# Softmax bias, scale and running minimum in one VectorE instruction per head, statistics of the last block one step later, last squares summed by TensorE

## The chip, the cores and the metric

The kernel runs on one core of a Trainium2 chip. The metric is the device time of one execution in microseconds (us). The engines are TensorE (PE in the profile, with PEld for its weight loads), VectorE (DVE), ScalarE (ACT), GpSimd (POOL) and SyncE (SP), which issues most of the transfers.

## The reference

One decoder layer on x of 2048 tokens by 1024 features, with three parallel mixers and a squared-ReLU MLP:

```python
proj = rmsnorm(x, norm1) @ w_in          # q|k|v|B|C|hc|p, 1792 columns
# attention, 8 heads of 64, 2 key heads, window 128, queries in blocks of 128
scores = einsum('bnqhgd,bnkhd->bnhgqk', qb, k_band) * scale        # 256 keys a block
scores = where(valid, scores + bias, NEG)
m = maximum(max(scores, axis=-1), sink)
p = exp(scores - m)
probs = p / (sum(p, axis=-1) + exp(sink - m))
attn = einsum('bnhgqk,bnkhd->bnqhgd', probs, v_band)
x = x + concat(attn, conv_out, pool_out) @ w_out
x = x + square(relu(rmsnorm(x, norm2) @ w1)) @ w2                  # d_ff 4096
return rmsnorm(x, final_norm)
```

All of it is float32.

## The kernel before

Everything is held transposed, features on the 128 partitions and tokens along the row. Every large matmul is three matmuls: each operand is split into a rounded high part and the rest (`hi`, `lo`), and `mm3` (L274 to L276) adds hi·hi, lo·hi and hi·lo in PSUM. A cast makes the high part (ACT) and a subtraction the low one (DVE or POOL), so splits run beside all stages.

Stage A goes over four blocks b of 512 tokens. A block projects x in 14 tiles (`pj_0` to `pj_13`, 24 matmuls each), runs attention, convolution (`cy`, `bo`) and pooling (`po`, `ppm`), writes the mixers' results split into `mxh` and `mxl`, and multiplies them by `w_out` (PE tiles also named `po`). Attention is done in eight units (j, g): 128 queries j and the four heads of key head g. `att_scores` puts a unit's scores into PSUM (`sc`, L577 and L578), and then, in SBUF tile `s` (128 x 4 x 257, the last column holding the sinks): scale and bias by DVE (L581), the negated maximum `nm` by DVE (L588), four exponentials by ACT with their sums `den` (L590), the reciprocal `rd` (L593) and the scaling (L594) by DVE. `att_trans` turns `s` by PE (L604, `pt`) into split tiles `pth`, `ptl`; `att_av` multiplies by the values (L615 and L616, `av`); `att_out` adds and splits the result (`ao`, L624, L629). The transposes `pt` share two PSUM banks with `ppm` and with the statistics.

Then norm2: squares of x are summed over features in `acc`, a matmul with `ones` sums them over partitions (`pst`), a few small DVE instructions form the inverse root (`rstd_of`), and the row is broadcast. Its last block stands in stage B, the first MLP product. Stage B multiplies in seven products, as in Strassen's scheme (named B11, T2, B21, T3, T1, T4, B22, with operands `hh` and `hl`, T or B), for 16 steps q; `on((q, product, place), f)` hangs other work to a place in it. Stage C is the second product, the residual sum and the final norm; its last half tile of 256 columns ends in `final_square`, `final_rstd`, `final_bcast`, `final_mul`. The final squares of a feature tile are made by ACT (L1136) and added to `acc` by POOL.

A scheduler with a timeline of its own sets the order of the instructions on each engine from dependences, pools and issue order, so an edit in one place can move others.

Of the kernel before, what the change touches and what calls it, by code (L numbers as in the profile page):

```python
# [20 lines left out]
P = 128  # L21
# [4 lines left out]
NB = S // T  # L26
HD = 64
NH = 8
# [8 lines left out]
ELEN = 384  # L37
# [15 lines left out]
PSK = PIC + 32  # L53
# [6 lines left out]
TM, TH = 2 * T, T  # L60
# [24 lines left out]
def tile_trunk(  # L85
# [14 lines left out]
    pe, act, dve, gp, sp = nc.tensor, nc.scalar, nc.vector, nc.gpsimd, nc.sync  # L100
# [11 lines left out]
    raw_src, plan, late = [], [], []  # L112
# [188 lines left out]
    def tmp(name):  # L301
        return pB.tile([P, T], F32, tag="tmp", name=name, bufs=4)
# [3 lines left out]

        return [min(o, w - P) for o in range(0, w, P)]

    def rstd_of(acc, r, offs, psp, tag, name):

        n = r.shape[-1]
        ps = psp.tile([P, T], F32, tag=tag, name=f"pst_{name}")
        for j, o in enumerate(offs):
            pe.matmul(ps[:, j : j + 1], acc[:, o : o + P], ones, start=True, stop=True)
        v, y, t = [cst.tile([P, 6], F32, tag=f"n{a}", name=f"n{a}_{name}", bufs=2)[:, :n] for a in "vyt"]
        dve.tensor_scalar(out=t, in0=ps[:, :n], scalar1=EPS, scalar2=None, op0=ALU.add)
        dve.tensor_scalar(out=v, in0=ps[:, :n], scalar1=EPS, scalar2=-0.5, op0=ALU.add, op1=ALU.mult)
        dve.tensor_scalar(
            out=y.bitcast(I32), in0=t.bitcast(I32), scalar1=-0.5, scalar2=1597463007.0,
            op0=ALU.mult, op1=ALU.add,  # L320
        )
        for it in range(3):
            dve.tensor_tensor(out=t, in0=y, in1=y, op=ALU.mult)
            dve.tensor_tensor(out=t, in0=t, in1=v, op=ALU.mult)
            dve.scalar_tensor_tensor(
                out=(r if it == 2 else y), in0=t, scalar=1.5, in1=y, op0=ALU.add, op1=ALU.mult
            )
# [86 lines left out]
    def load_bias():  # L414
        gp.memset(oh, 0.0)
        gp.memset(rl, 1.0)
        act.dma_start(oh[0 : NBUCKET + 1], oneh)
        act.dma_start(rl[0:NBUCKET], rel)

    def build_bias():  # L420

        for h in range(NH):
            ps = ps_tr.tile([P, T], F32, tag="tr", name=f"pse{h}")
            pe.matmul(ps[:, :ELEN], rl[:, h : h + 1].to_broadcast([P, P]), oh, start=True, stop=True)
            e = tmp(f"e{h}")[:, :ELEN]
            act.copy(e, ps[:, :ELEN])
            sp.dma_start(esc[h], e)

    def skew_bias():
# [9 lines left out]
    for k in range(KC):  # L439
        norm_load(0, k)  # L440
        if k in (0, 2, 4):
            w_load()
            if k < 4:
                w_load()
    load_bias()
    make_identity(nc, ident)
    for k in range(KC + 2):
        if k < KC:
# [120 lines left out]
    def att_scores(b, j, g):  # L569
        k0 = P if (b == 0 and j == 0) else 0  # L570
        n = 2 * P - k0
        sc = ps_sc.tile([P, 4, 2 * P], F32, tag="sc", name=f"sc{b}_{j}_{g}")
        for m in range(4):
            q = Q[b, 2 * g + m // 2]
            w = q[:, m % 2, j * P : (j + 1) * P]
            c = j * P + k0
            pe.matmul(sc[:, m, k0:], w, Kd[:, 2 * g, c : c + n], start=True, stop=False)  # L577
            pe.matmul(sc[:, m, k0:], w, Kd[:, 2 * g + 1, c : c + n], start=False, stop=True)  # L578
        s = pA.tile([P, 4, 2 * P + 1], F32, tag="s", name=f"s{b}_{j}_{g}", bufs=2)
        gp.tensor_copy(s[:, :, 2 * P], prm[:, PSK + 4 * g : PSK + 4 * g + 4])  # L580
        dve.scalar_tensor_tensor(  # L581
            out=s[:, :, k0 : 2 * P], in0=sc[:, :, k0:], scalar=1.0 / math.sqrt(HD),
            in1=bias[:, 4 * g : 4 * g + 4, k0:], op0=ALU.mult, op1=ALU.add,
        )
# [3 lines left out]
        dve.tensor_reduce(out=nm, in_=s[:, :, k0:], op=ALU.max, axis=AX.X, negate=True)  # L588
        for m in range(4):
            act.activation(  # L590
                s[:, m, k0:], s[:, m, k0:], AF.Exp, bias=nm[:, m : m + 1], accum_out=den[:, m : m + 1]
            )
        dve.reciprocal(out=rd, in_=den)  # L593
        dve.tensor_tensor(  # L594
            out=s[:, :, k0 : 2 * P], in0=s[:, :, k0 : 2 * P], in1=rd.unsqueeze(2).to_broadcast([P, 4, n]), op=ALU.mult
        )
        return b, j, g, s
# [145 lines left out]
    def norm2_row(b, psp, tag, t):  # L743
        row_store(rstd2[:, 4 * b : 4 * b + 4], "n2", b * T, T, psp, tag, f"n2_{b}", t)
# [187 lines left out]
    def um(name):  # L932
        return pT.tile([P, TH], F32, tag="u", name=name, bufs=18)
# [99 lines left out]
    def on(key, f, *a):  # L1033
        ev.setdefault(key, []).append(lambda: f(*a))

    for o in OPS[NEARLY:]:
        norm2_take(0, o)
    on((0, 0, 2), norm2_rstd, NB - 1, psb, "b")
    on((0, 1, 4), lambda: norm2_row(NB - 1, psb, "b", um("row2")))
    on((0, 3, 0), norm2_bcast, 1)  # L1040
    for k in range(HC):
        on((0, 4 + 2 * k, 0), norm2_blocks, 1, k, 0)
        on((0, 4 + 2 * k, 4), norm2_blocks, 1, k, 1)
# [81 lines left out]
    def y_of(p, f, n, cs):  # L1125
        return y[p, (11, 12, 21, 22)[2 * (f % 2) + n]][:, f // 2, cs]

    def final_square(p, n, f, cs, first):

        if first:  # L1130
            acc3[p, n] = pG.tile([P, TH], F32, tag="acc", name=f"acc3_{p}_{n}", bufs=3)
            act.activation(acc3[p, n][:, cs], y_of(p, f, n, cs), AF.Square)
            return
        w = cs.stop - cs.start
        sq = pG.tile([P, TH], F32, tag="sq", name=f"sq_{p}_{n}_{f}_{cs.start}", bufs=2)[:, :w]
        act.activation(sq, y_of(p, f, n, cs), AF.Square)  # L1136
        add(acc3[p, n][:, cs], acc3[p, n][:, cs], sq, gp)

    def final_rstd(p, n, cs):
        w = cs.stop - cs.start  # L1140
        offs = starts(w)
        r = cst.tile([P, 6], F32, tag="nr3", name=f"r3_{p}_{n}_{cs.start}", bufs=2)[:, : len(offs)]
        rstd_of(acc3[p, n][:, cs], r, offs, psb, "b", f"n3_{p}_{n}_{cs.start}")
        r3[p, n, cs.start] = r

    def final_bcast(p, n, cs):
        w = cs.stop - cs.start
        rb3[p, n, cs.start] = bcast(r3[p, n, cs.start], w, psb, "b", f"n3_{p}_{n}_{cs.start}")

    def final_mul(p, n, f, cs):  # L1150
        t = y_of(p, f, n, cs)
        dve.scalar_tensor_tensor(
            out=t, in0=t, scalar=prm[:, PGF + f : PGF + f + 1], in1=rb3[p, n, cs.start], op0=ALU.mult, op1=ALU.mult
        )
        a = p * TM + n * TH
        late.append(lambda: sp.dma_start(outT[f * P : (f + 1) * P, a + cs.start : a + cs.stop], t))

    ev = {}
    full = slice(0, TH)
# [66 lines left out]
            run(i)  # L1226

    cs = slice(TH // 2, TH)
    for j in range(HC):
        final_square(1, 0, 2 * j + 1, cs, False)  # L1230
    final_rstd(1, 0, cs)
    final_bcast(1, 0, cs)
    for f in range(KC):
        final_mul(1, 0, f, cs)
        flush()

    for st in (t2, t1, sZ, sY, sG):
# [77 lines left out]
```

## Time and profile before

| what | value |
|---|---|
| median of three runs | 1938.3 us (1936.6 to 1938.41) |
| the profiled execution | 1936.93 us |
| its span in the profile | 1935.2 us |
| TensorE clock granted, mean | 0.990 |
| instructions | 25620 |
| PE busy | 1892.6 us, 98% |
| DVE, ACT, POOL busy | 1123.6, 895.9, 1020.0 us |

Rows of the timeline give the start, the duration, the engine, the line of the kernel, the operation, output and inputs, and a count; a bracket holds the idle time ahead and what ended it. An operation in a group with xN lasts the printed time for all N. Matmuls overlap, so a row's duration is longer than the distance to the next: a 512-wide matmul is followed by the next 0.23 us later. Stage A lasts from the start to about 650 us, stage B and stage C from there to the end. Where the granted clock is 0.50, matmuls take twice as long.

### The profile page before, as it was taken

The numbers are of one execution on the slowest core, as the hardware profiler recorded it, in microseconds if no ns is written. First come the engines' busy times: TensorE is split into PE (matmuls) and PEld (weight loads), VectorE is DVE, ScalarE is ACT, GpSimd is POOL, SyncE is SP. The second block draws the span as 40 slices with busy tenths as digits, with TensorE's granted clock in tenths as the row PEclk, the third lists the DMA queues.
The fourth block names the chain that finished last, engine by engine and source line by source line (L and its number), as shares of the span: only waits on it lengthen the run. The fifth ranks groups of instructions, "written<-read, shape, count | busy, mean of one in ns | idle before, by whom it ended". The sixth has DMA issues, their size and how long they took to land.

```text
span 1935.2 us, 25620 instructions
## 1 busy us (share of the span) xinstructions
PE 1892.6 (98%) x8507; PEld 1527.8 (79%) x8507; DVE 1123.6 (58%) x1423; ACT 895.9 (46%) x1640; POOL 1020.0 (53%) x748
## 2 busy tenths in 40 slices
PE   8999999999899999999999999999999999999997
PEld 5877887887687788888888888888888888888887
DVE  5785686585888577756574444442425264533465
ACT  5664674564367344554575545442323222225332
POOL 5666557565463655654464444434565665526521
PEclk9999999999899999999999999999999999999998
DMA  7327316425935779756685655578777566645344
GB/s 255 102 65 225 108 61 217 126 66 174 300 117 178 233 272 335 255 197 212 216 288 194 196 185 189 186 270 279 235 231 240 191 218 200 221 123 169 96 158 134
DMA packets 194136, 373.34 MB, mean 193 GB/s; under 512 B 22167, under 2 KB 30420, under 8 KB 194004
## 3 DMA queue, kind: packets, MB, share of 16 engines
q1 hardware_dynamic: 193768, 371.62, 59.6%
q8 instruction: 67, 1.10, 0.2%
q14 instruction: 65, 0.53, 0.1%
q10 hardware_dynamic: 236, 0.09, 0.0%
HBM read 248.41 MB, written 116.93 MB: 189 GB/s over the span
## 4 chain that ended last, share of the span: by engine, by line
PE 83%; DVE 7%; DMA 6%; issue 2%; ACT 1%; POOL 1%; SPq 1%; DVEq 0%; POOLq 0%; ACTq 0%
PE o L274 11%; PE o L275 11%; PE o L276 11%; PE bT L275 6%; PE bT L276 6%; PE bT L274 6%; PE bB L275 5%; PE bB L274 5%; PE bB L276 5%; PE pj L275 4%; PE pj L276 4%; PE pj L274 4%; DMA x1s<-xo 1%; PE pt L604 1%; DVE xl L406 1%
## 5 line engine op out<-in xcount | busy, mean ns | idle before, releaser
L253 POOL TENSOR_TENSOR wl<-wr,wh 128x512 fp32r<-128x512 f32 x354 | 499.2, 1417 | 502.4 <-ACT wh L252 462.1
L252 ACT CAST wh<-wr 128x512 fp32r<-128x512 f32 x416 | 254.3, 617 | 362.5 <-PE bT L275 66.9
L763 DVE TENSOR_TENSOR bl<-br,bh 128x1024 fp32r<-128x1024 f32 (+2 forms) x144 | 186.8, 1300 | 324.7 <-ACT bh L1111 323.8
L275 PE MATMUL o<-bl,wh 128*128 128x512 f32 (+1 forms) x960 | 363.4, 381 | 0.0
L276 PE MATMUL o<-bh,wl 128*128 128x512 f32 (+1 forms) x960 | 362.7, 381 | 0.0
L274 PE MATMUL o<-bh,wh 128*128 128x512 f32 (+1 forms) x960 | 351.1, 381 | 0.0
L275 PEld LDWEIGHTS o<-bl,wh 128*128 128x128 f32 x960 | 180.9, 188 | 38.3 <-DVE bl L763 0.2
L276 PEld LDWEIGHTS o<-bh,wl 128*128 128x128 f32 x960 | 180.8, 188 | 38.2
L274 PEld LDWEIGHTS o<-bh,wh 128*128 128x128 f32 x960 | 176.3, 188 | 38.0
L276 PE MATMUL bT<-hhT,wl 128*128 128x512 f32 x512 | 203.7, 398 | 0.0
L275 PE MATMUL bT<-hlT,wh 128*128 128x512 f32 x512 | 203.6, 398 | 0.0
L274 PE MATMUL bT<-hhT,wh 128*128 128x512 f32 x512 | 203.4, 398 | 0.0
L274 PE MATMUL pj<-xh,wh 128*128 128x512 f32 x440 | 176.7, 403 | 10.6 <-ACT wh L252 6.7
L275 PE MATMUL pj<-xl,wh 128*128 128x512 f32 x440 | 177.5, 403 | 6.1 <-DVE xl L406 5.8
L276 PE MATMUL pj<-xh,wl 128*128 128x512 f32 x440 | 176.2, 401 | 0.0
L253 POOL TENSOR_TENSOR wl<-s,wh 128x512 fp32r<-128x512 f32 x64 | 91.2, 1426 | 141.5 <-ACT wh L252 130.9
L252 ACT CAST wh<-s 128x512 fp32r<-128x512 f32 x64 | 39.7, 621 | 250.1 <-PE o L275 249.9
L275 PE MATMUL bB<-hlB,wh 128*128 128x512 f32 x384 | 152.3, 397 | 0.7 <-DVE hlB L967 0.7
L274 PE MATMUL bB<-hhB,wh 128*128 128x512 f32 x384 | 152.5, 397 | 0.0
L1111 ACT CAST bh<-br 128x1024 fp32r<-128x1024 f32 (+2 forms) x144 | 123.2, 857 | 63.3 <-PE o L276 57.6
L276 PE MATMUL bB<-hhB,wl 128*128 128x512 f32 x384 | 152.0, 396 | 0.0
L220 POOL TENSOR_TENSOR s<-wr,wr 128x512 f32<-128x512 f32 x64 | 128.5, 2008 | 14.9 <-DMA wr<-in_w_dram 10.2
(188 smaller groups left out, 3388.0 us busy)
## 6 DMA issues: line engine op xcount, KB each, us to landing
wr<-in_w_dram SPq DMA_DIRECT2D x256, 256.0 KB, 3.8
hop_T<-s SPq DMA_DIRECT2D x128, 256.0 KB, 3.1
wr<-in_win_dram SPq DMA_DIRECT2D x112, 256.0 KB, 4.4
hop_B<-h SPq DMA_DIRECT2D x96, 256.0 KB, 3.3
br<-hop_B SPq DMA_DIRECT2D x48, 512.0 KB, 4.4
br<-hop_T SPq DMA_DIRECT2D x48, 512.0 KB, 4.3
wr<-in_wout_dram SPq DMA_DIRECT2D x64, 256.0 KB, 2.9
wr<-ss_T SPq DMA_DIRECT2D x48, 256.0 KB, 2.8
```

The lines of the kernel that those rows point to most:

```text
L220: gp.tensor_tensor(out=t, in0=a, in1=b, op=op)
L252: act.copy(hi, src)
L253: eng.tensor_tensor(out=lo, in0=src, in1=f32(hi), op=ALU.subtract)
L274: pe.matmul(ps, hi, xh, start=first, stop=False)
L275: pe.matmul(ps, hi, xl, start=False, stop=False)
L276: return pe.matmul(ps, lo, xh, start=False, stop=last)
L406: dve.tensor_tensor(out=xl[:, k], in0=hf, in1=f32(xh[:, k]), op=ALU.subtract)
L604: pe.transpose(ps[:, m * P : (m + 1) * P], s[:, m, kh * P : (kh + 1) * P], ident)
L763: return dve.tensor_tensor(out=out, in0=a, in1=b, op=ALU.subtract)
L1111: mark["act"] = act.copy(hi, src)
```

## The change

Three edits, and what follows from them:

1. In `att_scores`, one fused DVE instruction per head computes (score + 8·bias)·(−1/8) and, with it, the minimum over the row, seeded with the negated sink. It replaces the unit's scale-and-bias and its maximum. `s` then holds negated scores, and the exponential has `scale=-1`. The bias is stored times 8 (an ACT copy with a scale), and the negated sinks `nsink` are made once at the start by POOL.
2. The norm2 statistics of the last block are hung to later places of stage B.
3. In the tail, the four last squares stay in tiles `sql`, and PE adds them with `acc` in PSUM, instead of POOL. The last eight stores alternate between the queues of SP and ACT.

```diff
-    def rstd_of(acc, r, offs, psp, tag, name):
+    def rstd_of(accs, r, offs, psp, tag, name):
         ps = psp.tile([P, T], F32, tag=tag, name=f"pst_{name}")
+        accs = accs if isinstance(accs, list) else [accs]
         for j, o in enumerate(offs):
-            pe.matmul(ps[:, j : j + 1], acc[:, o : o + P], ones, start=True, stop=True)
+            for i, acc in enumerate(accs):
+                pe.matmul(ps[:, j : j + 1], acc[:, o : o + P], ones, start=i == 0, stop=i == len(accs) - 1)
...
-            act.copy(e, ps[:, :ELEN])
+            act.activation(e, ps[:, :ELEN], AF.Copy, scale=math.sqrt(HD))
...
+    nsink = cst.tile([P, NH], F32, name="nsink")
+    gp.tensor_scalar(out=nsink, in0=prm[:, PSK : PSK + NH], scalar1=-1.0, scalar2=None, op0=ALU.mult)
...
-        gp.tensor_copy(s[:, :, 2 * P], prm[:, PSK + 4 * g : PSK + 4 * g + 4])
-        dve.scalar_tensor_tensor(
-            out=s[:, :, k0 : 2 * P], in0=sc[:, :, k0:], scalar=1.0 / math.sqrt(HD),
-            in1=bias[:, 4 * g : 4 * g + 4, k0:], op0=ALU.mult, op1=ALU.add,
-        )
+        gp.tensor_copy(s[:, :, 2 * P], nsink[:, 4 * g : 4 * g + 4])
...
-        dve.tensor_reduce(out=nm, in_=s[:, :, k0:], op=ALU.max, axis=AX.X, negate=True)
         for m in range(4):
+            h = 4 * g + m
+            dve.tensor_tensor_reduce(
+                out=s[:, m, k0 : 2 * P], in0=sc[:, m, k0:], in1=bias[:, h, k0:], scale=-1.0 / math.sqrt(HD),
+                scalar=nsink[:, h : h + 1], op0=ALU.add, op1=ALU.min, accum_out=nm[:, m : m + 1],
+            )
             act.activation(
-                s[:, m, k0:], s[:, m, k0:], AF.Exp, bias=nm[:, m : m + 1], accum_out=den[:, m : m + 1]
+                s[:, m, k0:], s[:, m, k0:], AF.Exp, bias=nm[:, m : m + 1], scale=-1.0, accum_out=den[:, m : m + 1]
             )
...
-    on((0, 0, 2), norm2_rstd, NB - 1, psb, "b")
-    on((0, 1, 4), lambda: norm2_row(NB - 1, psb, "b", um("row2")))
-    on((0, 3, 0), norm2_bcast, 1)
+    on((0, 1, 2), norm2_rstd, NB - 1, psb, "b")
+    on((0, 2, 4), lambda: norm2_row(NB - 1, psb, "b", um("row2")))
+    on((0, 3, 2), norm2_bcast, 1)
...
-    def final_mul(p, n, f, cs):
+    def final_mul(p, n, f, cs, eng=sp):
...
-        late.append(lambda: sp.dma_start(outT[...], t))
+        late.append(lambda: eng.dma_start(outT[...], t))
...
+    w = TH // 2
+    acc3[1, 0] = [acc3[1, 0]]
     for j in range(HC):
-        final_square(1, 0, 2 * j + 1, cs, False)
+        if j % 2 == 0:
+            sq = pG.tile([P, TH], F32, tag="sq", name=f"sql_{j}", bufs=2)
+        t = sq[:, j % 2 * w : j % 2 * w + w]
+        act.activation(t, y_of(1, 2 * j + 1, 0, cs), AF.Square)
+        acc3[1, 0].append(t)
     final_rstd(1, 0, cs)
     final_bcast(1, 0, cs)
     for f in range(KC):
-        final_mul(1, 0, f, cs)
+        final_mul(1, 0, f, cs, act if f % 2 else sp)
         flush()
```

What stands in a row on an engine moves with it. The first place is the end of attention in the last block (b = 3), on DVE. The names end in numbers of the buffers; `s_3_1` is the unit of the last queries and the second key head. Before:

```order
L608 TENSOR_TENSOR ptl_1_1_0_5915<-pt_1_1_0_5909,pth_1_1_0_5914 128x512
L581 SCALAR_TENSOR_TENSOR s_3_1_5962<-sc_3_1_5953,bias 128x4x256
L624 TENSOR_TENSOR ao_0_1_5849<-av_0_1_5838,ao_0_1_5849 64x512
L608 TENSOR_TENSOR ptl_1_1_1_5924<-pt_1_1_1_5918,pth_1_1_1_5923 128x512
L588 TENSOR_REDUCE nm_3_1_5965<-s_3_1_5962 128x4
L629 TENSOR_TENSOR mxl<-ao_0_1_5849,mxh 64x4x128
L253 TENSOR_TENSOR wl_6167<-wr_5907,wh_6166 128x512
L593 RECIPROCAL rd_3_1_5967<-den_3_1_5966 128x4
L594 TENSOR_TENSOR s_3_1_5962<-s_3_1_5962,rd_3_1_5967 128x4x256
L708 SCALAR_TENSOR_TENSOR mxl<-ppm_0_5982,prm,mxh 128x512
```

And now, from the last of the unit's four pairs on:

```order
L592 ISA s_3_1_6026,nm_3_1_6028<-sc_3_1_6017,bias,nsink 128x256
L592 ISA nm_3_1_6028 128x1
L614 TENSOR_TENSOR ptl_1_1_1_5988<-pt_1_1_1_5982,pth_1_1_1_5987 128x512
L635 TENSOR_TENSOR mxl<-ao_0_1_5911,mxh 64x4x128
L599 RECIPROCAL rd_3_1_6030<-den_3_1_6029 128x4
L600 TENSOR_TENSOR s_3_1_6026<-s_3_1_6026,rd_3_1_6030 128x4x256
L714 SCALAR_TENSOR_TENSOR mxl<-ppm_0_6048,prm,mxh 128x512
```

A unit has eight instructions on DVE in place of two, the fused one (ISA, 128x256) and a read of its accumulator (128x1) for each head; `ptl_1_1_0`, `bo_0` and `ao_0_1` stand ahead of the first of them, and no weight split (`wl`) is between.

The same unit on PE: its last two score matmuls, before and now. `pj_11` is the projection tile ahead of `pj_7`.

```order
L577 MATMUL sc_3_1_5953<-Kd,q_3_5417 128x256
L578 MATMUL sc_3_1_5953<-Kd,q_3_5417 128x256
L274 MATMUL pj_7_6147<-xh_4866,wh_5903 128x512
L275 MATMUL pj_7_6147<-xl_4867,wh_5903 128x512
L276 MATMUL pj_7_6147<-xh_4866,wl_5904 128x512
```

```order
L582 MATMUL sc_3_1_6017<-Kd,q_3_5471 128x256
L583 MATMUL sc_3_1_6017<-Kd,q_3_5471 128x256
L275 MATMUL pj_11_6132<-xl_4917,wh_5864 128x512
L276 MATMUL pj_11_6132<-xh_4916,wl_5865 128x512
L274 MATMUL pj_11_6132<-xh_4916,wh_5864 128x512
```

Before, they stand ahead of the first matmul of `pj_7`; now they stand between the first and the second matmul of `pj_11`, a projection tile earlier.

The second place is the end of attention in the first block (b = 0), on PE: `pt_2_1_1` and `pt_3_1_0` are transposes of the last two units, `po_0` and `po_1` tiles of the output projection. Before:

```order
L615 MATMUL av_1_1_1335<-pth_1_1_0_1310,VV 128x512
L616 MATMUL av_1_1_1335<-ptl_1_1_0_1311,VV 128x512
L615 MATMUL av_1_1_1335<-pth_1_1_1_1319,VV 128x512
L616 MATMUL av_1_1_1335<-ptl_1_1_1_1320,VV 128x512
L604 MATMUL pt_2_1_0_1415<-ident,s_2_1_1265 128x128
L274 MATMUL po_0_1590<-mxh,wh_1409 128x512
L274 MATMUL po_1_1641<-mxh,wh_1478 128x512
L604 MATMUL pt_2_1_1_1424<-ident,s_2_1_1265 128x128 x4
L275 MATMUL po_0_1590<-mxl,wh_1409 128x512
```

And now:

```order
L610 MATMUL pt_2_1_1_1442<-ident,s_2_1_1279 128x128 x4
L276 MATMUL pj_7_1555<-xh_361,wl_1410 128x512
L274 MATMUL pj_7_1555<-xh_361,wh_1409 128x512
L621 MATMUL av_2_1_1463<-pth_2_1_0_1438,VV 128x512
L622 MATMUL av_2_1_1463<-ptl_2_1_0_1439,VV 128x512
L275 MATMUL pj_7_1555<-xl_362,wh_1409 128x512
```

`pt_2_1_1` has moved from behind the first matmuls of `po_0` and `po_1` into the end of `pj_7`; in its old place stands `pt_3_1_0`. On DVE, `mxl` from `ppm_0` (L708, now L714), which frees the PSUM bank that `pt_2_1_1` takes, stands behind `po_1`, `ao_1_1`, `ptl_2_1_0` and a `z` that it stood ahead of.

The third place is the tail on PE. Before:

```order
L276 MATMUL o_1_2_17171<-bh_17444,wl_16660 128x256
L275 MATMUL o_1_3_17175<-bl_17445,wh_16659 128x256
L276 MATMUL o_1_3_17175<-bh_17444,wl_16660 128x256
L314 MATMUL pst_n_1_0_256_17502<-ones,acc_1_0_16728 128x1 x2
L356 MATMUL pbc_n_1_0_256_17520<-ident,r_1_0_256_17501 128x128 x2
```

And now, the last of it:

```order
L316 MATMUL pst_n_1_0_256_17562<-ones,acc_1_0_16794 128x1
L316 MATMUL pst_n_1_0_256_17562<-ones,sql_17555 128x1 x2
L316 MATMUL pst_n_1_0_256_17562<-ones,sql_17558 128x1 x2
L358 MATMUL pbc_n_1_0_256_17588<-ident,r_1_0_256_17561 128x128 x2
L1324 UNCONDITIONAL_BRANCH
```

Ten small sums stand there in place of two, for each of two columns one of `acc` and four of `sql`; the one of `acc` for the first column stands earlier, ahead of the last `o` matmuls.

More of the change, by code (lines that the diff above doesn't have):

```diff
@@ L1142, in final_rstd @@
         r = cst.tile([P, 6], F32, tag="nr3", name=f"r3_{p}_{n}_{cs.start}", bufs=2)[:, : len(offs)]
-        rstd_of(acc3[p, n][:, cs], r, offs, psb, "b", f"n3_{p}_{n}_{cs.start}")
+        a = acc3[p, n]
+        rstd_of([a[0][:, cs]] + a[1:] if isinstance(a, list) else a[:, cs], r, offs, psb, "b", f"n3_{p}_{n}_{cs.start}")
         r3[p, n, cs.start] = r
@@ L1155, in final_mul @@
         a = p * TM + n * TH
-        late.append(lambda: sp.dma_start(outT[f * P : (f + 1) * P, a + cs.start : a + cs.stop], t))
+        late.append(lambda: eng.dma_start(outT[f * P : (f + 1) * P, a + cs.start : a + cs.stop], t))
     ev = {}
```

## The prediction

> **What bounds the kernel now.** I read the share of each engine first, then stretches of the span, then TensorE's waits in them.
>
> ```profile
> span 1935.2 us, 25620 instructions
> PE 1892.6 (98%) x8507; PEld 1527.8 (79%) x8507; DVE 1123.6 (58%) x1423; ACT 895.9 (46%) x1640; POOL 1020.0 (53%) x748
> ```
>
> PE is busy for 98% of the span: 1935.2 − 1892.6 = 42.6 us are open. Where, the stretches say (columns: start:end, length, busy us of PE, PEld, DVE, ACT, POOL, granted clock, DMA share, GB/s).
>
> ```profile
> 515.00:600.00 85.00, 80.22 (x393) 65.53 (x394) 71.28 (x95) 51.68 (x127) 44.86 (x37) 0.95 0.46 151
> 700.00:1300.00 600.00, 600.00 (x2562) 482.26 (x2561) 348.94 (x452) 309.43 (x517) 290.16 (x201) 1.00 0.68 229
> 1300.00:1900.00 600.00, 600.00 (x2697) 488.50 (x2696) 261.69 (x248) 189.29 (x272) 312.15 (x195) 1.00 0.63 199
> ```
>
> From 700 to 1900 us PE has no gap at full clock. The change takes no 512-wide matmul away, so it wins nothing there. It can win only in the gaps before 700 us and in the tail. In 515–600, the end of the last attention block, PE lacks 4.8 us and DVE is the busiest helper: 71.28 of 85, 13.7 spare. These are PE's waits and the clock behind them:
>
> ```profile
> 584.90 0.50 PE L274 MATMUL pj<-xh,wh 128*128 128x512 f32 x1 [0.80 <-DVE bo L653]
> 593.45 0.66 PE L604 MATMUL pt<-ident,s 128*128 128x128 f32 x4 [0.64 <-DVE mxl L708]
> 596.05 0.77 PE L615 MATMUL av<-pth,VV 128*128 128x512 f32 x1 [1.94 <-DVE ao L624]
> 595.60:602.40 6.80, 6.35 (x19) 4.95 (x20) 5.87 (x10) 4.40 (x8) 1.28 (x1) 0.50 0.04 15
> ```
>
> The bracket is the wait and its releaser. Three waits on DVE sum to 0.80 + 0.64 + 1.94 = 3.38 us. After them the granted clock is 0.50 for 6.8 us; 6.35 busy us at half speed lose about 3.1. Together this place costs 6.5 us.
>
> The Trainium skill, "TensorE: Matmul & The Clock Gate", Part 1, has the clock halve after an idle window of about 3.4 us; the longest wait here is 1.94 us, so this trace does not agree. By that rule the 3.1 us would not hang on these gaps, and closing them would win at most 3.4, which would put my sum 1.6 us higher.
>
> **Scores, bias and minimum in one instruction.** Before, a unit (128 queries, 4 heads) runs one instruction L581 and one L588 on DVE, then four exponentials on ACT, a reciprocal and a scaling.
>
> ```profile
> 587.93 1.21 DVE L588 TENSOR_REDUCE nm<-s 128x4 f32<-128x1028 f32 x1
> 589.18 0.51 ACT L590 ACTIVATE s<-s,nm 128x257 f32<-128x257 f32 x1 [0.59 <-DVE nm L588]
> 589.69 0.50 ACT L590 ACTIVATE s<-s,nm 128x257 f32<-128x257 f32 x1
> 591.30 0.18 DVE L593 RECIPROCAL rd<-den 128x4 f32<-128x4 f32 x1 [0.70 <-ACT s L590]
> L581 DVE SCALAR_TENSOR_TENSOR s<-sc,bias 128x1024 f32<-128x1024 f32 x30 | 36.5, 1216 | 12.3 <-PE sc L578 12.0
> L588 DVE TENSOR_REDUCE nm<-s 128x4 f32<-128x1028 f32 x30 | 36.3, 1210 | 0.2
> 670.84 0.15 DVE L316 TENSOR_SCALAR nt_n<-pst_n 128x4 f32<-128x4 f32 x1
> 670.91 0.15 DVE L317 TENSOR_SCALAR nv_n<-pst_n 128x4 f32<-128x4 f32 x1
> 1928.27 3.22 DVE L1152 SCALAR_TENSOR_TENSOR y<-y,prm,pbc_n 128x256 f32<-128x256 f32 x8 [1.38 <-PE pbc_n L356]
> ```
>
> Removed per unit: 1.216 + 1.210 = 2.43 us of DVE. Added: four fused instructions of 128x256, each with a read of its accumulator (128x1); the trace has neither. For the fused one, L1152 (128x256, one PSUM input, a scalar pointer) is nearest: 3.22 / 8 = 0.40 us. For the read, L316 and L317 bound it: 0.07 us from start to start, 0.15 us as a full duration. So a pair costs 0.47 to 0.55 us, and to 1.3 as a far end, if 256 columns cost what L581 takes for 1024 (1.22 + 0.07). I take 0.5, near the lower end, since L1152 has the same shape: 2.0 us per unit, 0.4 less than before, hidden, as PE is the bound.
>
> What counts is latency. Before, the first exponential starts after both whole instructions: from L581's start to the reciprocal 2.43 + (591.30 − 589.18) + 0.04 of hand-over = 4.6 us. Now head 0's exponential starts after its own pair, ACT's pitch (589.69 − 589.18 = 0.51) keeps up with the pairs, and the reciprocal can start after 4 × 0.5 + 0.5 to 0.7 = 2.6 us. A unit gains 2 us if DVE takes it up at once. The exponential's sign costs nothing (it rides in `scale`); the eight scaled copies and `nsink` stand at the start, in place of equal copies and before any unit: 0, between 0 and +0.3 (two small instructions of 0.15).
>
> The scheduler also reorders. In block 3 unit 3_1's scores stand some 20 matmuls (4.7 us, at 600 / 2562 = 0.234 us for one) earlier on PE, and `bo_0` (awaited at 584.90) and `ao` (awaited at 596.05) stand ahead of the unit's DVE work. So the three waits lose their causes: 2 us of latency plus 4.7 us of lead against single waits of at most 1.94. What is late next is the DVE queue itself (the L594 scaling, `ptl`, `mxl` of L708); I leave 1.5 us for it and take −5.0, between −6.5 (all gone, clock too) and +1 (the waits as now, and one more of the smallest size here). The gain reaches the end since the next block's loads of x follow `out_proj`'s last matmuls and the MLP has no slack to eat it.
>
> **The end of block 0** has the same kind of cluster.
>
> ```profile
> 120.13 0.66 PE L604 MATMUL pt<-ident,s 128*128 128x128 f32 x4 [1.85 <-DVE mxl L708]
> 128.47 0.50 PE L275 MATMUL ppm<-pol,pwh 128*128 128x512 f32 x1 [0.51 <-POOL pol L699]
> 136.84 0.50 PE L275 MATMUL po<-mxl,wh 128*128 128x512 f32 x1 [0.83 <-POOL mxl L655]
> 119.99 1.88 DVE L688 SCALAR_TENSOR_TENSOR po<-ps,prm,pp 64x512 f32<-64x512 f32 x2
> 121.90 0.69 DVE L624 TENSOR_TENSOR ao<-av,ao 64x512 f32<-64x512 f32 x1
> 121.20:128.00 6.80, 5.75 (x16) 3.19 (x14) 4.99 (x11) 3.06 (x6) 1.01 (x2) 0.50 0.13 39
> ```
>
> These waits are 3.2 us, the half clock 5.75 / 2 = 2.9: 6.1. The first is on `mxl` of L708, which frees the PSUM bank that the transposes `pt_2_1_1` need. On DVE two `po`, an `ao`, a `ptl` and a `z` now stand ahead of it: 1.88 + 3 × 0.69 = 3.95 us more, against 2 us of latency and 2 us of lead of the last scores. So `mxl` is done when it was, while the transposes come some nine matmuls (2 us) earlier on PE: that wait could grow to 1.85 + 2 = 3.9, and what PE did ahead of it is left for after it, where it covers the later waits. Taken 0, between −6.1 and +4 (the wait grows, the later ones stay, and the clock stays low 4 us longer). In blocks 1 and 2 the transposes also come earlier, by about 4 us of PE work (counted in matmuls of 0.234 between a unit's last score and its first transpose) against 2 us of saved latency. One pair of rows bounds the room, the end of a scaling and the transposes that need it:
>
> ```profile
> 574.37 1.21 DVE L594 TENSOR_TENSOR s<-s,rd 128x1024 f32<-128x1024 f32 x1
> 581.18 0.60 PE L604 MATMUL pt<-ident,s 128*128 128x128 f32 x4
> ```
>
> 581.18 − 575.58 = 5.6 us of slack, 3.6 left: 0.
>
> The waits at the start of block 3 are on loaded and split x, which the change does not touch; they stay:
>
> ```profile
> 489.29 0.80 PE L275 MATMUL pj<-xl,wh 128*128 128x512 f32 x1 [2.88 <-DVE xl L406]
> ```
>
> **Block 3's norm2 statistics a step later.**
>
> ```profile
> 658.17 1.05 PE L314 MATMUL pst_n<-ones,acc 128*128 128x1 f32 x8 [1.24 <-POOL acc L732]
> 660.50:663.90 3.40, 3.40 (x9) 2.62 (x9) 1.21 (x2) 1.79 (x4) 0.00 (x0) 0.50 0.94 305
> 662.54 1.53 DVE L967 TENSOR_TENSOR hlT<-xu_T,hhT 128x512 fp32r<-128x512 f32 x2 [6.79 <-ACT hhT L966]
> 670.97 0.50 PE L275 MATMUL bB<-hlB,wh 128*128 128x512 f32 x1 [0.73 <-DVE hlB L967]
> 670.98 0.68 DVE L967 TENSOR_TENSOR hlB<-xu_B,hhB 128x512 fp32r<-128x512 f32 x1
> ```
>
> Removed here: the wait of 1.24 and 3.4 / 2 = 1.7 us of half clock; the sums themselves (1.05) come back a product later. But behind them PE takes the products of T4 and B22, whose operands `hlT`, `hlB` DVE makes from 662.5 to 671.66 as loads come in, and PE already waits 0.73 for one. If PE comes 2.9 us earlier it waits there 2.9 longer. Taken 0, between −2.9 and +1.7 (the longer wait costs a second such clock window). The row and broadcast that follow have all of the next steps' matmuls to hide under.
>
> **The tail.**
>
> ```profile
> 1919.52 1.42 DVE L942 TENSOR_TENSOR y<-o,y 128x256 f32<-128x256 f32 x4 [2.70 <-PE o L276]
> 1920.04 0.75 ACT L1136 ACTIVATE sq<-y 128x256 f32<-128x256 f32 x2 [3.67 <-DVE y L942]
> 1920.53 3.12 POOL L942 TENSOR_TENSOR acc<-sq,acc 128x256 f32<-128x256 f32 x4 [19.09 <-ACT sq L1136]
> 1923.71 1.02 PE L314 MATMUL pst_n<-ones,acc 128*128 128x1 f32 x4 [3.52 <-POOL acc L942]
> 1928.78 3.77 SPq L1156 DMA_DIRECT2D out_dram<-y  x8
> ```
>
> The sum over features waits for POOL's four adds, until 1923.65. They go. The last `y` is there at 1919.52 + 1.42 = 1920.94; a square by ACT takes 0.75 / 2 = 0.38, so the squares are ready at about 1921.4. Then PE has the last one of column 0 and five of column 1: six matmuls, at 1.05 / 4 = 0.26 (L314 at 658, eight records for four matmuls) to 1.02 / 2 = 0.51 (here): 1.6 to 3.1 against 1.0 now. Gain 2.3 − 0.6 … 2.1: −1.7 to −0.2; I take −1.4, by the smaller pitch, since five stand in a row. The eight stores: SP issues them 3.77 / 8 = 0.47 apart, DVE finishes one per 0.40, and the last goes out at 1932.55, 1.06 after DVE's last at 1931.49. With ACT taking every second one only one issue is left behind DVE: −0.6, between −1.0 and 0 (ACT is no faster, and the landing still ends it). Tail: −2.0, between −2.7 and −0.2.
>
> **Sum.** −5.0 + 0 + 0 − 2.0 = −7.0 us. The profiled execution took 1936.93 (1.7 us around the span), 1.4 below the median 1938.3 of the three runs. 1938.3 − 7.0 = 1931.3.
>
> **Rivals.** Main: block 3's waits go, 1931.3; by its own ends (−6.5 to −2 there, the tail, some of block 0) 1926 to 1934.4. Chance 0.55.
>
> Gain returned, 0.23: DVE (71.28 of 85 us busy there) is as late as before, other waits of the same size take the place of the three, or a gap keeps the clock low. Only the tail is left: 1938.3 − 2 = 1936.3, 1934.5 to 1939. For it: every wait of the cluster is on DVE, and DVE gains just 0.4 us per unit. Against it: the waits are on late instructions, not on a saturated engine.
>
> Everything closes, 0.08: block 0 and norm2 too, −7.0 − 6.1 − some = about 1924.
>
> Slower, 0.14: the fused instruction is dear. Place: DVE in 515–600 has 13.7 us spare over 8 units, 1.7 each. The pairs eat that from 4p = 2.43 + 1.7, so from p = 1.0 us on. At the far end of 1.3 a unit is 5.2 − 4.1 = 1.1 us beyond DVE's time; over the 24 units of blocks 1 to 3 PE waits 26 us, less the tail: about 1962; at 1.1 still 24 × 0.3 = 7, less 2: 1943. Against it: L1152's 0.40 for the same elements.
>
> The Trainium skill, "VectorE: DVE Perf Modes", Rules for kernel authors, speaks for this rival: it advises against fusing chained DVE operations for speed, since the pipe drains after each one, and for a small count of operations, and here 2 become 8. Of that rule this trace shows a mild form only: L317 starts 0.07 us after L316, which lasts 0.15.
>
> That a fused instruction does nothing at all for PE, since scores were never awaited, is inside the second case.
>
> **Numbers.** A measurement tells about 0.2% (3.9 us) from no change: 1934.4 and 1942.2 are the borders. Faster: 0.53 of the main case and the 0.08, 0.61. Same: the other 0.02 and the 0.23, 0.25. Slower: 0.14. The range 1923 to 1941 takes in the first three cases and leaves out dear fusion and the best of "everything": under 0.2.
>
> **What would show it.** Per unit eight DVE rows of L592, the large ones near 0.4 us, 4 pairs in 2.0 us, and reciprocals 2.6 us after the first (wrong: pairs over 1 us). At block 3's end no wait on `bo`, `mxl`, `ao` over 0.5 us and no 0.50 window (wrong: 3 us of other waits, on `s` or `mxl`). Around 658 no wait on `acc`, but 2 to 3 us on `hlT` or `hlB` (wrong: none, then 2.9 more are won). In the tail PE's last sums start 0.5 us after DVE's last `y` (2.8 now) and no POOL add stands between (wrong: over 1.5 us). From 700 to 1900 the same 1200 us of PE: a longer MLP stretch would make all of this wrong.

## The result, and the profile after

The changed kernel takes 1919.46 us (median of four runs, 1915.52 to 1921.64) against 1938.11 before: 18.6 us less, a ratio of 0.990 (95% interval 0.9887 to 0.9914). The forecast was 1931.3, range 1923 to 1941: the direction held, the size did not.

The head of the profile after:

```profile
span 1916.8 us, 25848 instructions
PE 1877.0 (98%) x8523; PEld 1521.6 (79%) x8523; DVE 1115.7 (58%) x1615; ACT 896.1 (47%) x1640; POOL 1017.6 (53%) x745
```

PE's open time is 39.8 us, 2.8 less than before, but its busy time fell by 15.6 us, though its large matmuls are the same. A busy engine became shorter. The three stretches that the prediction showed of before, now of after (columns as there):

```profile
515.00:600.00 85.00, 82.78 (x416) 67.88 (x417) 74.52 (x147) 56.79 (x136) 44.63 (x37) 1.00 0.46 154
700.00:1300.00 600.00, 599.50 (x2574) 483.57 (x2573) 348.19 (x442) 306.97 (x510) 285.77 (x199) 1.00 0.68 232
1300.00:1900.00 600.00, 600.00 (x2775) 492.21 (x2774) 266.15 (x276) 188.59 (x276) 310.02 (x193) 1.00 0.62 196
```

In 700–1300 PE has 0.5 us of gaps more than before and the same clock, yet 2574 matmuls fit where 2562 did: 0.2329 us apart instead of 0.2342. (The last stretch also has the end moved into it, so its count isn't comparable.) This is the term that the prediction did not have.

In 515–600 the clock is 1.00 instead of 0.95. The fused scores of the last unit of block 3, in the timeline of after:

```profile
574.22 0.48 DVE L592 CUSTOM_DVE_ANT_0 s<-sc,bias,nsink 128x256 f32<-128x256 f32 x1
574.63 0.08 DVE L592 DVE_READ_ACCUMULATOR2_ANT nm<- 128x1 f32 x1
574.63 0.48 DVE L592 CUSTOM_DVE_ANT_0 s<-sc,bias,nsink 128x256 f32<-128x256 f32 x1
575.07 0.52 ACT L596 ACTIVATE s<-s,nm 128x257 f32<-128x257 f32 x1 [0.22 <-POOL s L585]
576.96 0.19 ACT L596 ACTIVATION_READ_ACCUMULATOR s<-s,nm 128x1 f32 x1
577.28 0.18 DVE L599 RECIPROCAL rd<-den 128x4 f32<-128x4 f32 x1
```

A pair costs 0.41 us from start to start; the read of the accumulator starts at the same instant as the next fused instruction and adds no time of its own in these rows. So a unit takes 1.64 us of DVE against 2.43 before (forecast 2.0). The reciprocal comes 3.06 us after the first pair (forecast 2.6): the first exponential starts 0.85 us after it, not 0.5, the sum of the fourth is read at 577.15, and two DVE instructions that stand between end at 577.25.

PE's waits at the places of the prediction, and the clock around them:

```profile
121.23 0.51 PE L621 MATMUL av<-pth,VV 128*128 128x512 f32 x1 [1.20 <-ACT pth L613]
125.87 0.50 PE L621 MATMUL av<-pth,VV 128*128 128x512 f32 x1 [1.43 <-DVE ao L630]
530.15 1.06 PE L610 MATMUL pt<-ident,s 128*128 128x128 f32 x8 [0.89 <-DVE s L600]
532.52 0.39 PE L582 MATMUL sc<-Kd,q 128*128 128x256 f32 x1 [0.85 <-DVE nm L592]
619.87 0.48 PE L274 MATMUL po<-mxh,wh 128*128 128x512 f32 x1 [1.35 <-DVE xo L730]
654.24 0.50 PE L275 MATMUL bT<-hlT,wh 128*128 128x512 f32 x1 [0.72 <-DVE hlT L973]
657.63 0.50 PE L275 MATMUL bB<-hlB,wh 128*128 128x512 f32 x1 [1.28 <-DVE hlB L973]
659.32 0.50 PE L275 MATMUL bB<-hlB,wh 128*128 128x512 f32 x1 [0.72 <-DVE hlB L973]
117.00:131.00 14.00, 10.31 (x44) 6.72 (x43) 11.43 (x20) 8.84 (x17) 6.97 (x8) 1.00 0.27 82
645.00:663.00 18.00, 14.71 (x58) 10.14 (x57) 11.41 (x14) 9.33 (x18) 10.89 (x8) 1.00 0.79 271
```

At the end of block 3 the waits on `bo`, `mxl` and `ao` are gone (0.42 on `ao` is left); new ones of 0.89 and 0.85 stand earlier in that block, and one of 1.35 on `xo` later. At the end of block 0, from 117 to 137 us, PE waits 3.7 us on other things (the two longest waits are shown), against 4.1 and 5.7 in the two profiles of before. After norm2 the wait on `acc` has turned into waits on `hlT` and `hlB`. Neither of these two places has a low clock any more.

The tail:

```profile
1903.57 1.42 DVE L948 TENSOR_TENSOR y<-o,y 128x256 f32<-128x256 f32 x4 [2.69 <-PE o L276]
1904.09 1.38 ACT L1242 ACTIVATE sql<-y 128x256 f32<-128x256 f32 x4 [3.67 <-DVE y L948]
1904.56 1.35 PE L316 MATMUL pst_n<-ones,sql 128*128 128x1 f32 x8 [0.32 <-ACT sql L1242]
1905.77 0.36 PE L316 MATMUL pst_n<-ones,acc 128*128 128x1 f32 x2
1905.99 1.03 PE L316 MATMUL pst_n<-ones,sql 128*128 128x1 f32 x8
1910.56 3.22 DVE L1159 SCALAR_TENSOR_TENSOR y<-y,prm,pbc_n 128x256 f32<-128x256 f32 x8 [1.38 <-PE pbc_n L358]
1911.07 2.68 SPq L1163 DMA_DIRECT2D out_dram<-y  x4
1911.47 2.69 ACTq L1163 DMA_DIRECT2D out_dram<-y  x4
```

From the first `y` to the end of PE's sums it was 1924.73 − 1919.52 = 5.21 us, now 1907.02 − 1903.57 = 3.45: 1.8 less (forecast 1.4). The last issue ends 0.38 us after DVE's last multiplication instead of 1.06: 0.7 less (forecast 0.6).

How far each kernel had come, in us of its own profile (the kernels are those of the next section; the last stretch is the tail):

| kernel | scores of block 3 | first MLP matmul | last `o` matmul | span | MLP alone |
|---|---|---|---|---|---|
| before | 516.1 | 648.3 | 1919.9 | 1935.2 | 1271.6 |
| before, second profile | 518.6 | 649.7 | 1922.0 | 1937.3 | 1272.4 |
| before + 32 bytes | 519.2 | 650.9 | 1914.5 | 1929.4 | 1263.6 |
| before + 96 bytes | 517.0 | 647.7 | 1893.3 | 1908.2 | 1245.6 |
| after, nothing moved | 508.8 | 635.0 | 1909.9 | 1922.7 | 1274.9 |
| after | 509.3 | 636.8 | 1904.0 | 1916.8 | 1267.1 |
| after, 96 bytes | 508.3 | 633.9 | 1881.0 | 1893.8 | 1247.1 |

And how long each block takes from its first scores to those of the next (block 3: to the first MLP matmul), with PE's gaps and the time at a clock of 0.50 in the four together:

| kernel | block 0 | block 1 | block 2 | block 3 | PE's gaps | at 0.50 |
|---|---|---|---|---|---|---|
| before | 148.6 | 151.1 | 164.0 | 132.2 | 19.2 | 23.9 |
| before, second profile | 147.9 | 152.4 | 165.7 | 131.0 | 23.7 | 13.7 |
| after, nothing moved | 144.9 | 150.1 | 161.4 | 126.3 | 12.4 | 13.7 |
| after | 144.5 | 150.4 | 161.8 | 127.6 | 18.0 | 6.8 |

### The profile page after: what moved, and what is told of

Its sections match the earlier page's. It is cut to its first block, busy times and chain, and to the rows that moved or that the text cites. A ratio compares the mean times of both kernels' runs of the same rounds, so it can differ in the third digit from the quotient of the medians.

```text
span 1916.8 us, 25848 instructions
## 1 busy us (share of the span) xinstructions
PE 1877.0 (98%) x8523; PEld 1521.6 (79%) x8523; DVE 1115.7 (58%) x1615; ACT 896.1 (47%) x1640; POOL 1017.6 (53%) x745
## 4 chain that ended last, share of the span: by engine, by line
PE 82%; DVE 8%; DMA 6%; ACT 2%; issue 2%; POOL 0%; SPq 0%; DVEq 0%; ACTq 0%; POOLq 0%
PE o L274 11%; PE o L275 11%; PE o L276 11%; PE bT L275 6%; PE bT L276 6%; PE bT L274 6%; PE bB L275 4%; PE bB L274 4%; PE bB L276 4%; PE pj L275 3%; PE pj L276 3%; PE pj L274 3%; PE po L275 1%; PE po L274 1%; PE po L276 1%
## 5 line engine op out<-in xcount | busy, mean ns | idle before, releaser
L252 ACT CAST wh<-s 128x512 fp32r<-128x512 f32 x64 | 39.8, 622 | 248.8 <-PE o L275 248.8
```

Of the source, the lines that this page charges most:

```text
L252: act.copy(hi, src)
```

## The experiments

**The three parts alone.** Each is the kernel before with that part of the diff and nothing else; on PE, each part moves just its own rows of the whole change.

> Only the fused scores of part 1 (with the exponential's sign, the bias times 8 and nsink); norm2 and the tail as before. Theory W (waits): the gain of the whole change is PE time that no longer waits on DVE in the four attention blocks; then this kernel gains 8 to 12 us, and PE's idle time ahead of 640 us falls from 27.5 us by at least 6. Theory C (clock): PE waits about as long as before, but in pieces that no longer pull the granted clock down; then it gains 8 to 12 us too, PE's idle time ahead of 640 us stays within 3 us of before, and the time at a clock of 0.50 ahead of 640 us falls from some 20 us to 10 or less. Theory P (placement): the MLP's matmuls run a trifle faster because of this part; then their distance between 700 and 900 us is 0.2335 us as in the changed kernel, otherwise 0.2342 as before.

Measured: 1920.44 us, ratio 0.9907 (0.9894 to 0.9919), 18 us less. The fused scores, with the tile that comes with them, bring nearly all, more than the step gave them. In 700–1300 us 2578 matmuls stand 0.2327 us apart (0.2342 before): theory P holds. Between W and C the run does not decide: ahead of 640 us PE is idle for 27.0 us, against 27.8 and 32.3 in the two profiles of before, and the clock is at 0.50 for 10.2 us, against 23.9 and 13.7. One execution of before has as waits what the other has as low clock.

> Only the later places of block 3's norm2 statistics. The prediction's step: the wait comes back on hlT and hlB, 0 us (within 1). Rival: it gains 2 to 3 us, since the low clock window behind the statistics goes and the waits on hlT and hlB are short. Theory P: if this part sets the pace of the MLP's matmuls, they are 0.2335 us apart between 700 and 900 us and the kernel gains 5 us more.

Measured: 1940.44 us, ratio 1.0009 (1.0000 to 1.0018): nothing won, +1.7. The wait comes back as the prediction had it, in the timeline of this kernel:

```profile
663.63 0.50 PE L275 MATMUL bT<-hlT,wh 128*128 128x512 f32 x1 [0.73 <-DVE hlT L967]
667.00 0.50 PE L275 MATMUL bB<-hlB,wh 128*128 128x512 f32 x1 [1.27 <-DVE hlB L967]
668.69 0.50 PE L275 MATMUL bB<-hlB,wh 128*128 128x512 f32 x1 [0.73 <-DVE hlB L967]
```

> Only the tail: last squares summed by PE, last eight stores from two queues. The prediction's step: 2.0 us faster, between 0.2 and 2.7; the changed kernel's profile suggests 2.5. Rival: the stores by ACT end no earlier and the gain is 1.5 or less.

Measured: 1936.0 us, ratio 0.9985 (0.9974 to 0.9996): 2.9 us less, 0.8 to 5.0.

> The kernel before, unchanged, as a second profile of it. Theory C: its low clock windows are not all at the same places as in the first profile, and its time moves with them by 2 to 4 us at most; a wait of about 2 us is followed by a low window and one of 1.4 is not. Theory P: the MLP's matmuls are 0.2342 us apart again; if instead they are 0.2335, the pace belongs to an execution and not to a kernel.

Measured: 1939.15 us, ratio 1.0005 (0.9995 to 1.0016). Matmuls 0.2343 apart again, so this pace isn't a matter of one execution. The low clock is: at the end of block 0 this execution has the wait of before (120.11 us) and no low clock. First the stretch ahead of the low clock in the first profile, then this one's rows:

```profile
117.80:121.20 3.40, 1.54 (x10) 1.02 (x9) 3.37 (x4) 1.48 (x3) 3.02 (x3) 0.99 0.19 70
```

```profile
120.11 0.66 PE L604 MATMUL pt<-ident,s 128*128 128x128 f32 x4 [1.85 <-DVE mxl L708]
119.20:122.60 3.40, 1.59 (x8) 1.07 (x8) 3.32 (x5) 0.59 (x1) 1.61 (x2) 1.00 0.22 67
121.20:128.00 6.80, 3.78 (x18) 2.24 (x17) 5.91 (x12) 3.57 (x7) 2.00 (x3) 1.00 0.12 39
```

What the 6.8 us of low clock cost, the same matmul behind the cluster shows, in the first profile and in this one:

```profile
129.90 0.47 PE L615 MATMUL av<-pth,VV 128*128 128x512 f32 x1
128.95 0.47 PE L615 MATMUL av<-pth,VV 128*128 128x512 f32 x1
```

From the transposes at 120.13 and 120.11 that is 9.77 us against 8.84: 0.9 us. At full clock PE waits longer there for `ao`, `ptl` and `pol`.

The low stretches of one execution begin at whole multiples of 3.413 us from each other (before: 121.2, 486.4, 517.1, 595.6, 660.5, 1923.4: 107, 9, 23, 19 and 370 of them), from a different start in each. Cut into such windows from 25 to 1890 us, the 18 profiles of this case have 55 in which PE idled 1.85 us or more, and 54 of them were followed by a low one; so were 18 of the 42 with 1.5 to 1.84 us, and 7 of the 81 with 1.0 to 1.5. The wait of 1.85 fell into one window whole in the first profile and was cut, 1.83 us of idle time in the window, in the second.

**The place of the buffers.** The new tile `nsink` lies ahead of the weights on the left side of SBUF and moves them, and all working buffers there, up by 32 bytes. These four kernels take place and change apart (in the traces PE, DVE and ACT of each kernel with an unused tile have the order of before, instruction for instruction):

```diff
  before + n bytes (n = 32, 64):
+    pad = cst.tile([P, n // 4], F32, name="pad")[:, :8]
+    gp.tensor_scalar(out=pad, in0=prm[:, PSK : PSK + NH], scalar1=-1.0, scalar2=None, op0=ALU.mult)
  after, nothing moved:
-    nsink = cst.tile([P, NH], F32, name="nsink")
+    nsink = prm[:, PSK : PSK + NH]           # negated in place
  after, 64 bytes:
+    nsink = cst.tile([P, 2 * NH], F32, name="nsink")[:, :NH]
```

> The kernel before with an unused tile of 8 floats (32 bytes of each partition) put where nsink stands in the changed kernel, written once by POOL. Every buffer of the left side of SBUF, the weights' high and low parts among them, moves up by 32 bytes, as it does in the changed kernel; the order of instructions on PE, DVE, ACT and SP is that of before. Theory P (placement): the MLP's matmuls stand 0.2323 to 0.2335 us apart instead of 0.2343, stage A's likewise, and the kernel gains 7 to 12 us. Theory S (the fused scores and the order that they bring): nothing changes, within 2 us, and the matmuls stay 0.2343 us apart.

Measured: 1931.77 us, ratio 0.9957 (0.9942 to 0.9973): 8.3 us less for an unused tile.

```profile
700.00:1300.00 600.00, 600.00 (x2583) 486.19 (x2583) 356.09 (x453) 309.84 (x519) 289.81 (x203) 1.00 0.69 230
```

2583 matmuls in the 600 us: 0.2323 us each.

> The changed kernel without the new tile: the sinks are negated in place, in the tile of parameters, so that every buffer stands where it stood before. Order on PE, ACT and SP as in the changed kernel. Theory P: the MLP's matmuls are 0.2343 us apart again, and of the 18.6 us only 7 to 11 are left (1927 to 1931 us). Theory S: still 1919 to 1921 us.

Measured: 1928.57 us, ratio 0.9946 (0.9930 to 0.9962): 10.5 us less. 2558 matmuls, 0.2342 us each:

```profile
700.00:1300.00 600.00, 599.14 (x2558) 481.38 (x2557) 345.01 (x441) 305.34 (x508) 281.92 (x198) 1.00 0.68 230
```

So the 18.6 us are about 8.3 of place and 10.5 of the rest, which add up within the intervals. Theory S falls.

> The changed kernel with a tile of 64 bytes for nsink in place of 32. If what counts is the place modulo 64 bytes, this equals the kernel with the sinks negated in place: 1927 to 1931 us and 0.2343 us from matmul to matmul. If it is the place modulo a larger number, another value, 1917 to 1931 us. Theory S: 1919 to 1921 us.

Measured: 1923.57 us, ratio 0.9920 (0.9908 to 0.9932), and

> The kernel before with an unused tile of 64 bytes. Modulo 64 bytes nothing moves: the time of before within 2 us and 0.2343 us from matmul to matmul. With a larger period it is another value. Theory S: the time of before.

1934.15 us, ratio 0.9975 (0.9963 to 0.9986). Three matmuls take 0.700 us in both. So 64 bytes is not like 0 bytes: the place has no period of 64.

**Which buffers, and how far.**

```diff
  before, 32 bytes on the right side:
+    pR = ctx.enter_context(tc.tile_pool(name="pR", bufs=1, side="right"))
+    pad = pR.tile([P, NH], F32, name="pad")   # written once by POOL, as above
  before + 96, + 128: pad of 24, 32 floats in cst
  weights + 96:
+    pad = wp.tile([P, 24], F32, tag="pad", name="pad", bufs=1)[:, :8]   # behind the raw loads
  after, 96 bytes:
+    nsink = cst.tile([P, 3 * NH], F32, name="nsink")[:, :NH]
```

> The kernel before with an unused tile of 32 bytes at the outer end of SBUF's right side, so that the operands that stream through PE (xh, xl, hh, hl, bh, bl) move down by 32 bytes while the weights stay. Order on PE, DVE, ACT and SP as before. In the MLP the weights were 32 bytes apart from these operands modulo 64 before; now the two stand alike, as they do with the weights moved up by 32. Theory R (the places relative to each other): three matmuls take 0.697 us as with the 32 bytes on the left, against 0.703 before, and 6 to 10 us are gained. Theory W (the weights' own place): 0.703 us and the time of before within 3 us. Theory M (the streamed operands' own place matters too): another value.

Measured: 1929.57 us, ratio 0.9949 (0.9930 to 0.9968): 9.9 us less, though nothing on the left moved. Three matmuls take 0.697 us up to a wait at 988.71 us and 0.700 behind it. That is no matter of the stage, nor of this pad: with the left side moved by 32 bytes, three of four profiles have the same two paces, in other stretches. First three stretches of `after` and the wait at which it turns faster, then the third stretch in before + 32 bytes, which keeps 0.697 (columns: start:end, length, busy us and matmuls of PE, clock, DMA share, GB/s):

```profile
720.00:960.00 240.00, 240.00 (x1030) 1.00 0.71 246
976.41 0.50 PE L275 MATMUL bT<-hlT,wh 128*128 128x512 f32 x1 [0.50 <-POOL hlT L973]
1000.00:1240.00 240.00, 240.00 (x1034) 1.00 0.59 196
1300.00:1540.00 240.00, 240.00 (x1031) 1.00 0.75 234
```

```profile
1300.00:1540.00 240.00, 240.00 (x1034) 1.00 0.76 242
```

At 1269.4 us, where stage C begins, `after` turns back to 0.700. So with the same places one kernel has two paces, some 5 us apart over a whole MLP (an estimate, 4 of 1034 of 1265 us); what picks one is open. Theory W falls. Theory R, whose gain of 6 to 10 us this is, fits as well as theory M: moving the weights up or the streamed operands down by 32 bytes gives the same two paces. Whether it is the distance between them that counts, a tile of 96 bytes on the right would tell; it was not run.

> The kernel before with an unused tile of 96 bytes on the left. Measured so far: 0 bytes 0.703 us for three matmuls, 32 bytes 0.697, 64 bytes 0.700. If the place modulo 64 and the place modulo 128 each count, 96 bytes give 0.697 or less and 7 to 12 us less than before; if the pace falls off with distance from 32, 0.703 and nothing gained.

Measured: 1910.83 us, ratio 0.9853 (0.9836 to 0.9871): 28 us less, with the instructions of the kernel before but for one small one of POOL's. Three matmuls take 0.687 us.

```profile
700.00:1300.00 600.00, 599.42 (x2616) 490.69 (x2615) 357.58 (x453) 313.04 (x523) 295.20 (x204) 1.00 0.70 235
```

> The kernel before with a tile of 96 bytes behind the ring of raw loads: the split weights (and the left side's working tiles behind them) move up by 96 bytes, while constants and raw loads stay. Theory W (the weights that PE loads): as with 96 bytes ahead of all, 1909 to 1913 us and 0.687 us for three matmuls. Rival (the raw loads, read by ACT, POOL and DVE, are what disturbs): 0.703 us and the time of before, or between.

Measured: 1911.52 us, ratio 0.9860 (0.9847 to 0.9874). Theory W, with one limit: the raw loads and constants stayed where they were, and the gain is the same, but the left side's working tiles behind the weights moved too, so that it is the weights alone isn't shown.

> The kernel before with an unused tile of 128 bytes on the left. If the place counts modulo 128 bytes: 0.703 us for three matmuls and the time of before within 2 us. If it counts modulo more, another value, 1905 to 1936 us.

Measured: 1933.33 us, ratio 0.9973 (0.9963 to 0.9983), 0.700 us for three matmuls: like 64 bytes, not like 0. So it isn't the place modulo 128 alone.

> The changed kernel with 96 bytes for nsink in place of 32, order as in the changed kernel. If place and the rest of the change simply add (place 96 bytes -28 us, the rest -10.5 us): 1898 to 1904 us, three matmuls of the MLP in 0.687 us. If they share a gain (the faster matmuls wait more often in the attention blocks): 1905 to 1911 us.

Measured: 1899.67 us, ratio 0.9800 (0.9787 to 0.9814), 38.9 us less than before. Place (28 us) and the rest (10.5) add.

**The rest of it.**

> The kernel before with the old two instructions issued head by head (scale and bias, then the maximum, 128x256 each), each head's exponential behind its own maximum; no new tile, sinks and signs as before. DVE's work per unit rises to about 4 x (0.40 + 0.33) = 2.9 us (2.43 before, 1.62 with the fused one). Theory L (the shorter way to the first exponential and the order that the scheduler makes of it bring the gain of the attention blocks): the end of block 3's attention comes 6 to 10 us earlier and the kernel gains 5 to 9 us. Theory D (DVE's time saved brings it): nothing gained or slower, -2 to +6 us.

Measured: 1936.77 us, ratio 0.9987 (0.9977 to 0.9997): 2.5 us less. Theory L falls. A unit takes 4 × (0.40 + 0.40) = 3.2 us of DVE (means of the groups of lines). Block 3's scores still came 3.6 us earlier than in the first profile (512.5 against 516.1), but from there to the MLP it took 131.7 us against 132.2: waits of 3.4 us are there, as before.

```profile
582.82 0.50 PE L274 MATMUL pj<-xh,wh 128*128 128x512 f32 x1 [1.58 <-DVE bo L653]
591.45 0.47 PE L615 MATMUL av<-pth,VV 128*128 128x512 f32 x1 [0.97 <-DVE ao L624]
593.63 0.82 PE L604 MATMUL pt<-ident,s 128*128 128x128 f32 x4 [0.82 <-DVE s L594]
```

So heads in turn, in the order that came of them, do not close them; in the changed kernel, where DVE's work is shorter, they close. As DVE's work rose here, the run does not tell order and DVE time apart, and what the DVE time does alone, in the old order, was not run.

> The changed kernel with the norm2 statistics of block 3 at their old places, all else as changed (buffers 32 bytes higher). The part alone measured +1.7 us (0 to +3.5) on the kernel before. If that holds here, 1917 to 1919.5 us; if the part is worth nothing, 1919.5; if it pays once attention ends earlier (the statistics waited 2.1 us in the kernel with the fused scores alone), 1920 to 1923.

Measured: 1915.96 us, ratio 0.9878 (0.9858 to 0.9898). The five executions spread from 1912.27 to 1924.17 us; the profile is of the last of these, which turned from 0.697 to 0.700 us for three matmuls at 981 us.

> As the changed kernel with 96 bytes, with the norm2 statistics of block 3 at their old places. With the changed kernel's 32 bytes this measured 3.5 us less, but the runs overlapped. If it holds: 2 to 4 us less than the kernel with 96 bytes; if the part is worth nothing, the same within 1.5 us.

Measured: 1896.56 us, ratio 0.9795 (0.9779 to 0.9811), the fastest of all; with the part it was 1899.67. In three pairs (+1.7, +3.5, +3.1 us) the later statistics never won. The first pair's interval touches zero and those of the other two overlap, so a loss is likely and not shown.

## Why the prediction was right or wrong

**What bounds the kernel, wrong.** "The change takes no 512-wide matmul away, so it wins nothing there" is the step that failed. It took the distance between two matmuls, 0.234 us, as a constant. It was the slowest that places on the left gave: three matmuls take 0.703, 0.697, 0.700, 0.687 and 0.700 us with the left side moved by 0, 32, 64, 96 and 128 bytes (with 32 bytes in some stretches 0.700). The new tile's 32 bytes were worth 8.3 us (5.2 to 11.2), nearly all in the MLP: 1263.6 us against 1271.6 in the table, while in stage A, whose blocks wait for loads, the moved kernels start the MLP no earlier. The prediction's last sentence, "the same 1200 us of PE", was the test that showed it. The edit that brought it was in the diff, priced as "two small instructions": what a tile does by its size was left out. That the place does it is shown by the kernels that differ from before in a tile and one small POOL instruction alone; why it does is open.

**Fused scores.** The pair was priced at 0.5 and is 0.41; the direction (hidden, but shorter) held. Block 3, forecast −5.0: from its scores to the MLP it takes 127.6 us in after and 126.3 with nothing moved, against 132.2 and 131.0 in the two profiles of before, so −3.5 to −5.9. This step was right, and its three waits went, though after has other waits in that block (0.89, 0.85 and 1.35 us).

Mis-sized was the term "taken 0" for blocks 0 to 2: the scores of block 3 start 7 to 10 us earlier than in the two profiles of before. All seven kernels with the fused scores start them at 507.1 to 512.7 us, all ten with the old two instructions as they were at 514.6 to 519.2. By the second table block 0 gave 3.1 to 4.1 us, block 1 0.8 to 2.3 and block 2 2.2 to 4.3. PE's gaps and half the time at 0.50, added over the four blocks, fall from 31.1 and 30.5 us to 19.2 and 21.4 (an estimate, since half the low time stands for its loss): most of the 12 to 14 us by which the four blocks are shorter. So the mechanism was the forecast one, waits and low clock that go, in more places than were counted; at the end of block 0 the prediction had also left out waits of 0.67 on `ao` and 0.27 on `ptl`. Which wait closes by which part of the change is not settled. Not all of it reached the end: with nothing moved PE's gaps in the MLP are 4.0 us, against 2.0 and 2.4 before, so "the MLP has no slack to eat it" held only in part.

**The clock.** The prediction charged 3.1 and 2.9 us to low windows and let them go with the waits. They are no fixed part of the kernel: before has 27 us of low clock ahead of 700 us in the first profile and 17 in the second, and the first is the shorter one, 1935.2 us against 1937.3. Their price was too high, as work at half clock takes the place of waits: at the end of block 0 it is 0.9 us, not 2.9. (Nor are matmuls twice as slow there: in the second profile of before they stand 0.43 us apart at 0.50, 672.7 to 675.2 us, against 0.234.) The changed kernel's profile had 7 us of low clock. What is worth doing is to keep the idle time of any 3.4 us under 1.5. The end of block 3 now does (0.42). Block 0 splits its waits, 1.20 and 1.43 with work between, which was enough in this execution; with nothing moved a window there had 1.68 us of idle time, and 3.4 us at 0.50 followed.

The Trainium skill, "TensorE: Matmul & The Clock Gate", Part 1, names a free-running window of about 3.4 us, and the traces agree with it; its other sentence, that the clock halves after an idle window, they do not bear out, as 1.85 idle us or more in such a window were enough in 54 of 55 cases.

**Norm2, right in the waits.** Those on `hlT` and `hlB` came (3.28 us in 650–660). In size it was taken 0 and measured +1.7 alone, at the upper end of its bounds, and about +3 with the rest of the change; the loss is not shown.

**The tail, right.** −2.0 forecast; −2.9 (−0.8 to −5.0) alone, and 2.5 in the two profiles.

**The rivals.** "Slower" needed a pair over 1.0 us; it is 0.41. Eight instructions took 0.8 us less than two. The advice of the Trainium skill ("VectorE: DVE Perf Modes", Rules for kernel authors) against fusing and for few operations does not fit this trace. "Gain returned" did not come about. Without the moved buffers the changed kernel gains 10.5 us, where 7.0 were forecast: by its own terms the forecast was 3.5 us off, mostly in blocks 0 to 2.

## What to carry to other kernels

Where PE is busy for nearly the whole span, look at the distance between its matmuls before looking at its gaps: here 2.3% of 1200 us hung on where the buffers lie, and a pad of 96 bytes (28 us) was worth more than the whole change (18.6). A new tile moves all those behind it, so an edit that adds one is measured against the old kernel with an unused tile of that size, or the edit gets the credit of the place. A term "taken 0" needs the same look as the large ones: those of blocks 0 to 2 held more together (7 to 10 us) than the term that was worked out (3.5 to 5.9). And when low clock windows follow waits, price them as a chance per execution, less the waits that they cover, not as a full cost of the wait.

## What the runs showed of the hardware

The pace of 512-wide matmuls depends on the SBUF places of their operands: from 0.229 to 0.2343 us from one to the next, with the left side (the weights and the working tiles behind them) moved by 0 to 128 bytes, or the right side (the streamed operands) by 32. A place need not fix it: with 32 bytes on either side an execution has 0.697 or 0.700 us for three matmuls, and changes between them. Why is open: no period of 64 or 128 bytes fits, and the place of the raw loads has no part in it. The accumulator's read behind a fused 128x256 instruction adds no time on DVE (0.41 us from pair to pair, and one such instruction lasts 0.48). Low stretches of the granted clock begin whole multiples of 3.413 us apart, with another start in each execution, and a window with 1.85 us or more of idle PE was followed by a low one in 54 of 55 cases.
